# A ninth tile done by quarters in both column halves of the first feed-forward's second product, second in the order of the second half

## The chip, the cores and the metric

The kernel runs on one core of one Trainium2 chip. The metric is the device time of one execution in microseconds (us); lower is better. Times shown are the median of three runs, and a profile of one further execution.

## The reference

One decoder layer on 512 tokens of width 1024: a SwiGLU feed-forward, a token mixer (HGRN2 and mLSTM heads), a second feed-forward, each between two RMS norms and with a residual. The change lies in the first feed-forward, after `silu(gate) * up`:

```python
def swiglu_ffn(x, w_in, w_out):
    gate, up = jnp.split(x @ w_in, 2, axis=-1)
    return (jax.nn.silu(gate) * up) @ w_out
...
  x = x + 0.5 * rms_norm(swiglu_ffn(rms_norm(x, norm_pre[l, 0]), ffn1_w_in[l], ffn1_w_out[l]),
                         norm_post[l, 0])
```

`ffn1_w_out` is 2816 x 1024. The second product is therefore (512 x 2816) by (2816 x 1024).

## The kernel before

**Numbers.** All products are of float32 data, split into two float32r parts: a high part, made by a cast on ScalarE (ACT), and a low part, what is left of the value, made by a subtraction on VectorE (DVE). A product of two such operands is three matmuls: high by high, high by low, low by high. Weights are split by `split` (line 294 the cast, line 296 the subtraction) into one of four buffers, `w`; activations by `two_parts` (lines 884 and 885).

**The second product** (`ffn_out`) takes the 2816 rows of the weights in eleven tiles of 256 rows, numbered 0 to 10, and the 1024 output columns in two halves of 512. `OUT` gives the order of the tiles in each half. A tile is done in one of two ways.

- Plainly (`plain`, line 1004): 48 matmuls of 128 x 256, one weight item. The activations are split by `h_tile` into a buffer of the ring `s`, which has three.
- By quarters (`quartered`, line 1012): the tile's 2 x 2 blocks are multiplied with seven block products in place of eight (Winograd's form of Strassen's algorithm), 42 matmuls. It takes two weight items: three of the four weight quarters (a split of 768 columns), and four sums of weight quarters. The activations need three quarters, split on their own (`h_quarters`), and four sums (`h_sums`, line 919, three DVE operations), split by `s_tile` into a buffer of the ring `s`. `QUARTERED` names the tiles done so in each half.

In a half, the seven products of all quartered tiles go to four accumulators common to them (`M`) and four of the output (`C`), eight PSUM banks in all. After the half's last quartered tile, `common` combines the four `M` banks with one ACT copy and four DVE operations (lines 1039 and 969), and `add` adds the results to `C`. After the first half, eight post steps on DVE (line 491) read `C` for the norm. In the second half the last four tiles of the order (`LAST`: 0, 1, 7 and 5) are done row block by row block, so that the norm of a row block can follow (`chunk`, `last`).

**The sums of weights** are made by DMA alone, in DRAM (`sums_ahead`): three copies issued by SyncE (SP; lines 938 to 940), then three accumulating DMAs issued by GpSimd (POOL; line 944), and are loaded like weights. `make_sums` begins one tile and takes each begun one a step further; it is called at every fifth product of the first feed-forward's first part from the fifteenth on, and then at every second tile of the second product's first half.

**Buffers of the activations' quarters.** Tiles 2, 4, 6 and 8 have places of their own (`PLACES`, in `xq`). Tile 3 keeps two of the three buffers of the ring `raw` from the first half until its turn in the second. Tiles 5, 7 and 9 follow each other in the third `raw` buffer and in `gpre`, high and low part. Tiles whose quarters are used in the second half too (`stay`) have their sums written in place over the activations `hf`; the others get them in `xn` (`hsum`). In the second half before, tile 9 is done plainly, seventh in the order. Tile 7's parts go over the places of 4 and 8 there (`LATER`). `more` makes the next tiles' parts ahead; at a plain tile in place seven of the second half it makes all that are left. The first weight load of the mixer uses the ring `raw`, and the next norm's gain uses `gpre`.

Each engine runs its instructions in order. The order on each engine is set by a scheduler that goes by the code's order and its own model; it is shown below where it moves.

Of the kernel before, what the change touches and what calls it, by code (L numbers as in the profile page):

```python
# [23 lines left out]
PAIRS = NF // 2  # L24
# [60 lines left out]


FIRST = (2, 3, 4, 5, 6, 7, 8, 9)
QUARTERED = {"f1": [FIRST, (2, 3, 4, 6, 8)], "f2": [FIRST, (2, 3, 4, 6, 8, 9, 5)]}
OUT = {"f1": [list(range(PAIRS)), [10, 2, 4, 3, 6, 8, 9, 0, 1, 7, 5]]}
OUT["f2"] = [OUT["f1"][0], [10, 2, 4, 3, 6, 8, 9, 5, 7, 0, 1]]  # L90
LAST, APART, TWICE = {"f1": 4, "f2": 2}, (5, 7, 9), (5, 9)
PLACES, LATER = {2: 1, 4: 2, 6: 0, 8: 3}, {7: (2, 3)}

AGAIN, ROWS = (10,), (18, 19, 20, 21)
EVERY, EARLY, AHEAD = 5, 7, 13
# [28 lines left out]
class Layer:  # L124
# [718 lines left out]
    def ffn_in(self):  # L843

        nc = self.nc
        if not self.second:
            self.begun = ()
            self.sums_due("f1")
        for n, (p, t) in enumerate(ORDER2[len(HEADS2) :] if self.second else ORDER[len(HEADS) :]):
            if n > 14 and n % EVERY == 0 and not self.second:  # L850
                self.make_sums()
            if n == 14 and self.second:

                with self.behind(self.pooled):
                    nc.gpsimd.drain()
            with self.behind(*(self.c22 if p in ("p3", "p5") and self.second else ())):
                self.feed()
            self.c22 = []
            self.lag()
            self.prod(p, t)  # L860
            self.after(p, t)
            if t == PAIRS - 1 and p in ("p3", "p7"):
                self.hs.append(self.h_tile(len(self.hs)))
            if n == 1 and not self.second:
                self.lower_bound()
        self.feed()
        self.lag()
# [96 lines left out]
    def ffn_out(self, gpost_row, scale, after, trans, head):  # L964
# [3 lines left out]
        nc, mm = self.nc, self.nc.tensor.matmul  # L968
        tt = lambda out, a, b, op: nc.vector.tensor_tensor(out, a, b, op=op)
        f = "f2" if self.second else "f1"  # L970
        OF, QF, LF = OUT[f], QUARTERED[f], LAST[f]
        low = self.low
        seq = [(half, k2) for half in range(2) for k2 in OF[half]]
        made = deque((h, None) for h in self.hs)
# [1 line left out]
        kept, again = {}, deque()  # L976

        def more(n):
            while count[0] < min(n, len(seq)):
                half, k2 = seq[count[0]]  # L980
                count[0] += 1
                if k2 in QF[half]:
                    if k2 not in kept or half and k2 in TWICE:
                        stay = k2 in QF[1] and k2 not in TWICE
                        a = self.h_quarters(k2, PLACES.get(k2))
                        with self.behind(*([] if stay else [low])):
                            kept[k2] = a, self.h_sums(k2, stay)
                    a, f = kept[k2]
                    made.append((a, self.s_tile(f)))
                elif half and k2 in AGAIN:  # L990
                    made.append(again.popleft())
                else:
                    made.append((self.h_tile(k2, self.x_place(*LATER[k2]) if half and k2 in LATER else None), None))
                    if not half and k2 in AGAIN:
                        again.append(made[-1])
# [63 lines left out]
        n = 0  # L1059
        for half in range(2):  # L1060
            C = [[self.ps() for _ in range(2)] for _ in range(2)]
            M, T, left = None, None, len(QF[half])
            for m, k2 in enumerate(OF[half][: PAIRS - LF * half]):
                more(n + 2)
                h, sums = made.popleft()
                if sums:
                    begin = M is None
                    if begin:
                        M = {p: self.ps() for p in ("p1", "p5", "p7", "p6")}

                    quartered(C, M, h, sums, begin, half and OF[1][m : m + 2] == list(TWICE)[::-1])
                    left -= 1
                    if left == 0:
                        T = common(M, [self.hf[:, j, :] for j in ROWS] if half else [self.st("c") for _ in range(4)])
                else:
                    w = self.pull()
                    more(len(seq) if half and m == PAIRS - LF - 1 else n + 3)
                    for i in (0, 2, 1, 3):
                        for v in range(2):
                            plain(C, w, h, i, v, m == 0)  # L1080
                        if i > 1 and T and m == PAIRS - 1:
                            add(C, T, i % 2)
                    self.drop(w)
                n += 1
                if half == 0 and n % 2:
                    self.make_sums()
                if n == 1:
                    self.prod("p4", PAIRS - 1)
                    self.after("p4", PAIRS - 1)
                self.lag()  # L1090
            if half == 0:
                ys = [self.post0(pieces(C, i), g, scale) for i in range(NT)]
                self.holes()
# [884 lines left out]
```

## Time and profile before

| | us |
|---|---|
| median of three runs | 914.87 (914.43 to 915.07) |
| the profiled execution, its own time | 914.82 |
| its span, first to last instruction | 913.1 |
| second product, first half and second half to the end of the eighth tile | 223.16 to 309.5 |
| tiles 7, 8, 9, 10 of the first half begin at | 260.56, 265.32, 270.08, 274.85 |
| tiles 2, 4, 3, 6, 8, 9 of the second half begin at | 285.73, 290.5, 295.25, 300.0, 304.8, 309.52 |
| first row block of tiles 0, 1, 7, 5 begins at | 314.96 |
| head of the mixer's products (L560) begins at | 338.85 |

Times inside are microseconds from the start of the span. TensorE is PE, its weight loads PEld. A row of the timeline gives the start, the length, the engine, the line, the operation, output and input by the program's names, and how many were merged; in brackets stands the idle time before it and what ended it. A row of grouped instructions gives the busy time, the mean length of one in ns, and the idle time before them. A row of stretches gives PE, PEld, DVE, ACT and POOL busy, the granted PE clock, the DMA engines' share and GB/s.

### The profile page before, as it was taken

Reading aid. Unit: us, or ns where it says so; the run is one execution under the profiler, and the core shown is the slowest. Engines: PE = TensorE matmul, PEld = TensorE weight load, DVE = VectorE, ACT = ScalarE, POOL = GpSimd, SP = SyncE. Lnnn points to the kernel's source line nnn. Section 1 sums busy time; section 2 is a strip of 40 time slices with the busy share of each in tenths; the row PEclk is TensorE's granted clock in tenths of the full one; section 3 lists DMA queues with packets and bytes.
Section 4 is the critical chain, followed back from the end, with each engine's and each line's share of the span. In section 5 each row is a group of like instructions: output and inputs, shape, how many; then the busy total and the mean of one; then the engine's idle time right before and its main releaser. Section 6 shows DMA issues by size and latency. Waiting matters only on the chain.

```text
span 913.1 us, 18148 instructions
## 1 busy us (share of the span) xinstructions
PE 904.7 (99%) x7330; PEld 874.7 (96%) x7330; DVE 767.1 (84%) x1005; ACT 522.3 (57%) x749; POOL 183.2 (20%) x256
## 2 busy tenths in 40 slices
PE   9999999999999999999999999999999999999997
PEld 8999999999999999998888888899999999999997
DVE  6899988889888876699986655699899889988886
ACT  7645545557566557857643345694445545757661
POOL 2541112121111047742230300313000000010002
PEclk9999999999999999999999999999999999999999
DMA  9355779775897825899953127053354445388542
GB/s 311 83 161 140 186 191 213 188 156 137 222 273 237 249 62 143 158 200 210 204 119 116 40 76 253 24 162 95 97 156 140 139 130 156 101 238 242 171 144 93
DMA packets 127921, 146.51 MB, mean 160 GB/s; under 512 B 16335, under 2 KB 100303, under 8 KB 127837
## 3 DMA queue, kind: packets, MB, share of 16 engines
q1 hardware_dynamic: 111868, 130.14, 46.8%
q0 software_dynamic: 15680, 14.69, 11.8%
q8 instruction: 57, 0.93, 0.4%
q10 hardware_dynamic: 288, 0.52, 0.2%
q14 instruction: 28, 0.22, 0.1%
HBM read 143.20 MB, written 31.48 MB: 191 GB/s over the span
## 4 chain that ended last, share of the span: by engine, by line
PE 62%; ACT 0%; DVE 0%; DVEq 0%; POOLq 0%; issue 0%; POOL 0%; ACTq 0%
PE ps L619 23%; PE ps L1012 8%; PE ps L549 6%; PE ps L198 5%; PE ps L200 5%; PE ps L199 5%; PE ps L1004 4%; PE ps L560 1%; PE ps L1441 1%; PE ps L364 1%; PE ps L1540 0%; PE ps L1742 0%; PE ps L1491 0%; PE ps L1715 0%; PE ps L1739 0%; PE ps L1505 0%
## 5 line engine op out<-in xcount | busy, mean ns | idle before, releaser
L294 ACT CAST w<-raw 128x1024 fp32r<-128x1024 f32 x246 | 250.9, 1027 | 190.6 <-PE ps L619 91.7
L296 DVE TENSOR_TENSOR w<-raw,w 128x1024 fp32r<-128x1024 f32 x246 | 299.4, 1221 | 30.7 <-ACT w L294 29.5
L619 PE MATMUL ps<-xq,w 128*128 128x256 f32 x2016 | 236.9, 277 | 0.0
L619 PEld LDWEIGHTS ps<-xq,w 128*128 128x128 f32 x2016 | 232.8, 188 | 0.0
L619 PE MATMUL ps<-sq,w 128*128 128x256 f32 x1512 | 177.6, 276 | 0.0
L619 PEld LDWEIGHTS ps<-sq,w 128*128 128x128 f32 x1512 | 174.2, 188 | 0.0
L310 DVE TENSOR_TENSOR raw<-raw,raw 128x1024 f32<-128x1024 f32 x72 | 89.8, 1252 | 7.1 <-DMA raw<-in_ffn_w_in_dram 5.6
L1012 PE MATMUL ps<-w,hs 128*128 128x256 f32 x672 | 80.9, 276 | 0.0
L1004 PE MATMUL ps<-w,hs 128*128 128x256 f32 x672 | 79.2, 276 | 0.0
L1012 PEld LDWEIGHTS ps<-w,hs 128*128 128x128 f32 x672 | 78.3, 188 | 0.0
L1004 PEld LDWEIGHTS ps<-w,hs 128*128 128x128 f32 x672 | 77.5, 188 | 0.0
L198 PE MATMUL ps<-w,xq 128*128 128x512 f32 x176 | 71.1, 404 | 0.0
L200 PE MATMUL ps<-w,xq 128*128 128x512 f32 x176 | 68.9, 392 | 0.0
L199 PE MATMUL ps<-w,xq 128*128 128x512 f32 x176 | 68.6, 390 | 0.0
L944 POOL DMA_DIRECT2D f2sums<-in_ffn_w_out_dram x15 | 20.2, 1522 | 178.6 <-DMA f2sums<-in_ffn_w_out_dram 178.1
L549 PE MATMUL ps<-xq,w 128*128 128x256 f32 x480 | 55.7, 278 | 0.0
L549 PEld LDWEIGHTS ps<-xq,w 128*128 128x128 f32 x480 | 54.9, 188 | 0.5 <-issue 0.5
L884 ACT CAST hs<-hf 128x1024 fp32r<-128x1024 f32 x32 | 33.7, 1053 | 27.4 <-PE ps L1012 19.7
L885 DVE TENSOR_TENSOR hs<-hf,hs 128x1024 fp32r<-128x1024 f32 x32 | 39.1, 1223 | 9.0 <-ACT hs L884 8.4
L944 POOL DMA_DIRECT2D f1sums<-f1sums x26 | 22.0, 847 | 108.6 <-DMA f1sums<-in_ffn_w_out_dram 57.4
L944 POOL DMA_DIRECT2D f2sums<-f2sums x30 | 26.3, 911 | 85.7 <-DMA f2sums<-in_ffn_w_out_dram 44.6
L310 POOL TENSOR_TENSOR raw<-raw,raw 128x1024 f32<-128x1024 f32 x12 | 32.6, 2722 | 40.9 <-DVE w L296 40.7
(263 smaller groups left out, 1234.2 us busy)
## 6 DMA issues: line engine op xcount, KB each, us to landing
raw<-in_ffn_w_in_dram SPq DMA_DIRECT2D x98, 512.0 KB, 4.7
raw<-in_ffn_w_out_dram SPq DMA_DIRECT2D x44, 512.0 KB, 5.5
raw<-in_w_mix_in_dram SPq DMA_DIRECT2D x28, 512.0 KB, 4.7
raw<-f2sums SPq DMA_DIRECT2D x15, 512.0 KB, 5.1
raw<-f1sums SPq DMA_DIRECT2D x13, 512.0 KB, 6.4
raw<-in_w_mix_out_dram SPq DMA_DIRECT2D x8, 512.0 KB, 4.3
f2sums<-in_ffn_w_out_dram SPq DMA_DIRECT2D x30, 128.0 KB, 4.9
f2sums<-in_ffn_w_out_dram SPq DMA_DIRECT2D x15, 256.0 KB, 6.4
```

Of the source, the lines that this page charges most:

```text
L198: mm(ps, sh, mh, start=start, stop=False, **kw)
L199: mm(ps, sh, ml, start=False, stop=False, **kw)
L200: mm(ps, sl, mh, start=False, stop=stop, **kw)
L294: nc.scalar.copy(hi, raw)
L296: self.low = nc.vector.tensor_tensor(lo, raw, hi.bitcast(F32), op=ALU.subtract)
L310: added = (nc.vector if late else nc.gpsimd).tensor_tensor(o, o, c, op=ALU.add)
L549: mm(ps[:, u0:u1], w[:, a, k, :], self.xop(k, b, u0, u1), start=k + n + m == 0, stop=k == ND - 1 and n == 2, skip_group_check=True,)
L619: self.nc.tensor.matmul(ps[:, c], wb[b][:, k, v], left[d][:, k, :], start=first and a + n + k == 0, stop=n == 2 and k == KH - 1, skip_grou ...
L885: self.nc.vector.tensor_tensor(lo, src, hi.bitcast(F32), op=ALU.subtract)
L944: nc.gpsimd.dma_start(to[:, a:b], v, accum_op=ALU.add)
L1004: mm(out, a[kk][:, i * P : (i + 1) * P], w[:, b, kk, QUARTER * v : QUARTER * (v + 1)], start=begin and c == kk == n == 0, stop=kk == 1 and ...
L1012: mm(ps[:, QUARTER * c : QUARTER * (c + 1)], A[a][:, c], B[b], start=begin and c == n == 0, stop=n == 2, skip_group_check=True,)
```

## The change

Tile 9 joins the tiles done by quarters in the second half of the first feed-forward, and stands second in its order. Its quarters and sums of the first half stay, so `TWICE`, the tiles made anew for the second half, becomes a table by feed-forward: none in the first, 5 and 9 in the second, as it was. There is one more tile of weight sums to make, and `make_sums` is called once more, at the tenth product.

```diff
-QUARTERED = {"f1": [FIRST, (2, 3, 4, 6, 8)], "f2": [FIRST, (2, 3, 4, 6, 8, 9, 5)]}
-OUT = {"f1": [list(range(PAIRS)), [10, 2, 4, 3, 6, 8, 9, 0, 1, 7, 5]]}
+QUARTERED = {"f1": [FIRST, (2, 3, 4, 6, 8, 9)], "f2": [FIRST, (2, 3, 4, 6, 8, 9, 5)]}
+OUT = {"f1": [list(range(PAIRS)), [10, 9, 2, 4, 3, 6, 8, 0, 1, 7, 5]]}
 OUT["f2"] = [OUT["f1"][0], [10, 2, 4, 3, 6, 8, 9, 5, 7, 0, 1]]
-LAST, APART, TWICE = {"f1": 4, "f2": 2}, (5, 7, 9), (5, 9)
+LAST, APART, TWICE = {"f1": 4, "f2": 2}, (5, 7, 9), {"f1": (), "f2": (5, 9)}
...
-            if n > 14 and n % EVERY == 0 and not self.second:
+            if n > 9 and n % EVERY == 0 and not self.second:
                 self.make_sums()
...
-        OF, QF, LF = OUT[f], QUARTERED[f], LAST[f]
+        OF, QF, LF, two = OUT[f], QUARTERED[f], LAST[f], TWICE[f]
...
-                    if k2 not in kept or half and k2 in TWICE:
-                        stay = k2 in QF[1] and k2 not in TWICE
+                    if k2 not in kept or half and k2 in two:
+                        stay = k2 in QF[1] and k2 not in two
...
-                    quartered(C, M, h, sums, begin, half and OF[1][m : m + 2] == list(TWICE)[::-1])
+                    quartered(C, M, h, sums, begin, half and OF[1][m : m + 2] == list(two)[::-1])
```

The order of instructions differs only between the first half's last tiles and the first row block of the last four tiles, and by the copies and accumulations of the added sums. Three places follow.

**DVE at the end of the first half, before.** `hs_3208` is the low part of tile 9's sums, `hs_3263` that of tile 10, `once_3199` the low parts of tile 9's quarters, `hs_3329` the low part of tile 2's sums for the second half; `raw_172` and `raw_173` are tile 9's two weight items, `raw_178` and `raw_179` tile 10's.

```order
L885 TENSOR_TENSOR hs_3208<-hsum_3204,hs_3208 128x1024
L296 TENSOR_TENSOR w<-raw_170_2980,w 128x1024
L296 TENSOR_TENSOR w<-raw_172_3024,w 128x768
L885 TENSOR_TENSOR hs_3263<-hf_113,hs_3263 128x1024
L885 TENSOR_TENSOR once_3199<-hf_113,once_3198 128x256
L885 TENSOR_TENSOR once_3199<-hf_113,once_3198 128x512
L296 TENSOR_TENSOR w<-raw_173_3046,w 128x1024
L296 TENSOR_TENSOR w<-raw_178_3087,w 128x1024
L885 TENSOR_TENSOR hs_3329<-hf_113,hs_3329 128x1024
L296 TENSOR_TENSOR w<-raw_179_3109,w 128x1024
```

The same place now; tile 9's sums are `hs_3214` in the first half and `hs_3335` for the second, tile 10 is `hs_3269`, tile 9's quarters are `once_3206`.

```order
L296 TENSOR_TENSOR w<-raw_170_2987,w 128x1024
L296 TENSOR_TENSOR w<-raw_172_3031,w 128x768
L885 TENSOR_TENSOR once_3206<-hf_114,once_3205 128x256
L885 TENSOR_TENSOR once_3206<-hf_114,once_3205 128x512
L919 TENSOR_TENSOR hf_114<-hf_114 128x2x128
L296 TENSOR_TENSOR w<-raw_173_3053,w 128x1024
L919 TENSOR_TENSOR hf_114<-hf_114 128x4x128
L296 TENSOR_TENSOR w<-raw_178_3094,w 128x1024
L885 TENSOR_TENSOR hs_3214<-hf_114,hs_3214 128x1024
L885 TENSOR_TENSOR hs_3269<-hf_114,hs_3269 128x1024
L296 TENSOR_TENSOR w<-raw_179_3116,w 128x1024
L885 TENSOR_TENSOR hs_3335<-hf_114,hs_3335 128x1024
```

The low part of tile 9's sums moved from ahead of its quarters to behind them, behind the second and third of the sums (L919) and behind two weight splits.

**DVE at the end of the second half, before.** L969 are the steps of `common`, then of `add`; `xq_77` is tile 7's low part, `hs_3774` that of tile 1, `hs_3779` that of tile 5, `raw_247` and `raw_249` the weights of 7 and 5.

```order
L969 TENSOR_TENSOR hf_113<-ps_3501,hf_113 128x512
L885 TENSOR_TENSOR xq_77<-hf_113,xq_76 128x1024
L969 TENSOR_TENSOR hf_113<-ps_3503,hf_113 128x512
L296 TENSOR_TENSOR w<-raw_247_3634,w 128x1024
L969 TENSOR_TENSOR hf_113<-hf_113,ps_3502 128x512
L885 TENSOR_TENSOR hs_3774<-hf_113,hs_3774 128x1024
L969 TENSOR_TENSOR hf_113<-ps_3501,hf_113 128x512
L969 TENSOR_TENSOR ps_3443<-ps_3443,hf_113 128x512
L969 TENSOR_TENSOR ps_3444<-ps_3444,hf_113 128x512
L885 TENSOR_TENSOR hs_3779<-hf_113,hs_3779 128x1024
L296 TENSOR_TENSOR w<-raw_249_3665,w 128x1024
```

Now, with `hs_3835` for tile 5, `raw_248` and `raw_249` for the weights of 7 and 5, and `ps_3449` and `ps_3450` for the accumulators of the second row block:

```order
L969 TENSOR_TENSOR ps_3450<-ps_3450,hf_114 128x512
L296 TENSOR_TENSOR w<-raw_248_3671,w 128x1024
L969 TENSOR_TENSOR hf_114<-ps_3507,hf_114 128x512
L885 TENSOR_TENSOR xq_77<-hf_114,xq_76 128x1024
L969 TENSOR_TENSOR hf_114<-ps_3509,hf_114 128x512
L296 TENSOR_TENSOR w<-raw_249_3693,w 128x1024
L969 TENSOR_TENSOR hf_114<-hf_114,ps_3508 128x512
L885 TENSOR_TENSOR hs_3835<-hf_114,hs_3835 128x1024
L969 TENSOR_TENSOR hf_114<-ps_3507,hf_114 128x512
L969 TENSOR_TENSOR ps_3449<-ps_3449,hf_114 128x512
L969 TENSOR_TENSOR ps_3447<-ps_3447,hf_114 128x512
```

The last two weight splits and tile 5's low part moved in between the steps of `common`. On PE, tile 5's four first matmuls of high parts (two for each column half) and two of tile 0 for the second row block now stand ahead of the first that reads tile 5's low part.

**SP's loads in the second half, before.** `raw_3736` is the mixer's first weight item, `gpre` the next norm's gain; `raw_190`, `raw_196` and `raw_240` are tiles 3, 6 and 8.

```order
L255 DMA raw_190_3268<-in_ffn_w_out_dram 128x2x512
L255 DMA raw_191_3290<-f1sums_3_92 128x1024
L255 DMA raw_3736<-in_w_mix_in_dram 128x8x128
L165 DMA gpre_3923<-in_norm_pre_dram 128x1024
L255 DMA raw_196_3327<-in_ffn_w_out_dram 128x2x512
L255 DMA raw_234_3447<-f1sums_6_93 128x1024
L255 DMA raw_240_3506<-in_ffn_w_out_dram 128x2x512
```

Now, with `raw_239` for tile 6 and `raw_242` for tile 8:

```order
L255 DMA raw_239_3512<-in_ffn_w_out_dram 128x2x512
L255 DMA raw_240_3534<-f1sums_6_94 128x1024
L255 DMA raw_3773<-in_w_mix_in_dram 128x8x128
L165 DMA gpre_3927<-in_norm_pre_dram 128x1024
L255 DMA raw_242_3565<-in_ffn_w_out_dram 128x2x512
L255 DMA raw_243_3587<-f1sums_8_95 128x1024
```

The mixer's first load and the gain moved from behind tile 3's loads to behind tile 6's, ahead of tile 8's.

## The prediction

> **What bounds the kernel now.** I read the page's busy line first, then TensorE's waits over the whole span, then busy time by stretches around the end of the first feed-forward.
>
> ```profile
> PE 904.7 (99%) x7330; PEld 874.7 (96%) x7330; DVE 767.1 (84%) x1005; ACT 522.3 (57%) x749; POOL 183.2 (20%) x256
> PE ps L194 <- POOL ones L172: 1.2, 1, 1.2
> PE ps L364 <- DVE xn L754: 0.5, 1, 0.5
> PE ps L619 <- ACT xq L384: 0.2, 1, 0.2
> 260.00:270.00 10.00, 10.00 (x91) 10.00 (x90) 7.97 (x9) 7.02 (x9) 2.01 (x2) 1.00 0.91 203
> 275.00:280.00 5.00, 5.00 (x47) 5.00 (x46) 4.89 (x7) 1.37 (x2) 0.42 (x1) 1.00 0.96 282
> 310.00:315.00 5.00, 5.00 (x47) 5.00 (x46) 5.00 (x6) 1.04 (x2) 0.00 (x0) 1.00 0.84 236
> ```
>
> PE is busy for 99% of the span and its longest listed wait is 1.2 us at the start. In the stretches (PE, PEld, DVE, ACT, POOL, clock, DMA share) it never rests while the second product runs, at clock 1.00. So a matmul removed there is worth its pitch, and any new PE wait costs its length; nothing else counts. DVE is nearly full at 275 to 280 and at 310 to 315: there a step that moves later on DVE can become a PE wait.
>
> **The matmuls.** The ninth tile of the second column half is done plainly now: 4 row blocks x 2 column halves x 2 contraction halves x 3 terms = 48 matmuls. By quarters it is 7 products of 6, 42.
>
> ```profile
> 274.85 11.04 PE L1004 MATMUL ps<-w,hs 128*128 128x256 f32 x96
> 285.73 1.52 PE L1012 MATMUL ps<-w,xq 128*128 128x256 f32 x12
> ```
>
> The 96 matmuls of the tenth tile (48 in each half) begin at 274.85 and the next group at 285.73: 10.88 us, 113 ns each. (The 276 ns in the groups is the length of one, not its pitch.) Six fewer save **0.68 us**. A plain tile takes 5.44 us, a quartered one 4.76.
>
> **First half: the sums of the ninth tile come later.** They are now written in place over its activations, so they must follow the casts of its quarters. These need the third `raw` buffer and `gpre`, which the seventh tile holds until its last matmul.
>
> ```profile
> 264.64 0.84 PE L1012 MATMUL ps<-w,once 128*128 128x256 f32 x6
> 270.08 1.52 PE L1012 MATMUL ps<-w,once 128*128 128x256 f32 x12
> 271.44 2.88 PE L1012 MATMUL ps<-w,hs 128*128 128x256 f32 x24
> ...
> 261.17 1.23 DVE L885 TENSOR_TENSOR hs<-hsum,hs 128x1024 fp32r<-128x1024 f32 x1 [0.59 <-ACT hs L884]
> 265.80 0.92 ACT L884 CAST once<-hf 128x256 fp32r<-128x256 f32 x2
> 267.08 1.02 DVE L885 TENSOR_TENSOR once<-hf,once 128x256 fp32r<-128x256 f32 x2
> 268.01 2.35 DVE L296 TENSOR_TENSOR w<-raw,w 128x1024 fp32r<-128x1024 f32 x2
> ...
> L919 DVE TENSOR_TENSOR hf<-hf 128x512 f32<-128x512 f32 x5 | 3.4, 693 | 0.1
> L919 DVE TENSOR_TENSOR hf<-hf 128x256 f32<-128x256 f32 x5 | 2.0, 423 | 0.1
> L884 ACT CAST hs<-hf 128x1024 fp32r<-128x1024 f32 x17 | 17.9, 1054 | 16.6 <-PE ps L1012 10.6 <-PE ps L1004 4.1 <-DVE hf L919 1.9
> L1012 PEld LDWEIGHTS ps<-w,hs 128*128 128x128 f32 x312 | 36.3, 188 | 0.0
> ```
>
> Before, their low part was done at 262.4, nine microseconds ahead of its use after 271.44. Now, in the new DVE order: the seventh tile ends at 265.48; ACT casts both pieces (0.92) to 266.4; the second low piece (about 0.69) to 267.1; the second sum (0.42, after a short handover) to 267.6; the sums' weight split (half of 2.35, so 1.17) to 268.75; the third sum (0.69) to about 269.4. Then ACT casts (1.05) to 270.4 while DVE does another split, to about 270.5; the low part (1.23) ends at 271.7. PE wants it for the third matmul after 271.44, at 271.67, and must first load it (188 ns). So the cover is gone: I take **0.2 us** of wait. It is bounded by 0 and by one further DVE operation of 1.22 in between, 1.4. PE then waits one for one, since all matmuls stand in one queue.
>
> Behind it DVE has 2.3 us of work (0.42 + 0.69 + 1.23) moved from before 263 into a full stretch. From 271.6 on come five operations of 1024 columns (1.14 each), a split of 768 (0.87) and four combination steps (0.65): the combination of the first half ends at about 280.7, and the adds to the accumulators start 1.2 us later than now, the eight post steps too.
>
> ```profile
> 279.49 2.48 DVE L969 TENSOR_TENSOR ps<-ps,c 128x512 f32<-128x512 f32 x4
> 281.87 3.65 DVE L491 TENSOR_TENSOR y<-ps,gpost 128x256 f32<-128x256 f32 x8
> ```
>
> The tenth tile's second pass asks for the first bank that the combination frees, already free when ACT has copied it, and for the last only 3.4 us (30 matmuls) after its start. At 285.7 to 285.9 the quartered part needs the first old accumulator; its last reader is the fifth of the eight post steps, ending at 281.87 + 1.2 + 5/8 of 3.65 = 285.35. I cost this at **nothing**; were the banks handed out from the other end, it would be 286.7 less 285.9, 0.8.
>
> **Second half: its end has lost the plain tile.** The combination used to run beside the plain ninth tile. Now the eighth tile takes that place in time, ends at 309.52 + 4.76 = 314.28, and the last four tiles follow at once.
>
> ```profile
> 309.52 8.32 PE L1004 MATMUL ps<-w,hs 128*128 128x256 f32 x72
> 319.04 2.88 PE L1004 MATMUL ps<-w,hs 128*128 128x256 f32 x24
> ...
> 309.83 1.22 DVE L885 TENSOR_TENSOR xq<-hf,xq 128x1024 fp32r<-128x1024 f32 x1
> 310.96 0.69 DVE L969 TENSOR_TENSOR hf<-ps,hf 128x512 f32<-128x512 f32 x1
> 316.25 1.23 DVE L885 TENSOR_TENSOR hs<-hf,hs 128x1024 fp32r<-128x1024 f32 x1
> ```
>
> The seventh tile's low part is written over the eighth's quarters, so it starts when the eighth ends: 309.83 before, 314.45 now, and all that stands behind it on DVE waits. In order: that (1.14 until the next can start) to 315.6, a combination step (2.48 / 4 = 0.62) to 316.2, the fifth tile's weight split (1.14) to 317.35, a step to 317.95, the fifth tile's low part (1.23) to 319.2. Before, that was ready at 317.5 and wanted at 319.04. Now PE has done tiles 0, 1 and 7 of the first row block (36 x 113 ns) at 318.36, four high-part matmuls and two of the next block by 319.04, and then needs it, loaded, at 319.4: **0.25 us** after a rounding down, since the first wait shifts both sides alike. The add that the next block needs comes after two more steps, at 320.5, when the 11 matmuls in between have just passed. Bounds: 0, and one more DVE operation late, 1.5.
>
> **Costed at nothing.** The extra weight item makes one more 768-wide split.
>
> ```profile
> L296 DVE TENSOR_TENSOR w<-raw,w 128x768 fp32r<-128x768 f32 x13 | 12.4, 955 | 1.4 <-ACT w L294 1.1
> L294 ACT CAST w<-raw 128x768 fp32r<-128x768 f32 x13 | 10.8, 834 | 4.5 <-PE ps L1012 2.1 <-ACT w L294 1.5 <-DMA raw<-in_ffn_w_out_dram 0.8
> 295.85 1.23 DVE L885 TENSOR_TENSOR hs<-hf,hs 128x1024 fp32r<-128x1024 f32 x1 [1.30 <-ACT hs L884]
> 64.78 0.60 SPq L940 DMA_DIRECT2D f1sums<-in_ffn_w_out_dram  x1
> 65.48 0.53 SPq L255 DMA_DIRECT2D raw<-in_ffn_w_in_dram  x1
> 74.73 0.37 SPq L255 DMA_DIRECT2D raw<-in_ffn_w_in_dram  x1
> 75.55 0.84 POOL L944 DMA_DIRECT2D f1sums<-f1sums  x1 [3.82 <-DMA f1sums<-in_ffn_w_out_dram]
> 85.61 2.48 DVE L310 TENSOR_TENSOR raw<-raw,raw 128x1024 f32<-128x1024 f32 x2
> raw<-in_ffn_w_out_dram SPq DMA_DIRECT2D x44, 512.0 KB, 5.5
> ```
>
> The split's 0.96 us on DVE and 0.83 on ACT fit the 1.30 that DVE idles within a quartered tile; without it, at most 0.96. The three more copies on SP stand between the loads at 65.48 and 74.73, a gap of 9 us for about 1.8 of issuing (0.60 each); the load ahead of them is first read at 85.6, 20 us after its issue, so sharing the DMA engines with them is harmless. POOL's three more accumulations (0.84 each) fall between waits of 3 us and more on DMAs; the other tiles' keep their places because the making of sums begins one call earlier. If this cover failed, a DVE wait of a few microseconds near 70 would meet a full DVE.
>
> **Sum.** 914.82 for the profiled execution (span 913.1 and 1.7 around it; the median shown is 914.87) - 0.68 + 0.2 + 0.25 = 914.6, a gain of 0.2 us.
>
> **Rivals.** A measurement of this kernel tells about 0.2% from no change, 1.83 us.
>
> A: both low parts come in time, because handovers are shorter than I took them: 914.82 - 0.68 = 914.1, and the same verdict. For it: each lateness is some 0.2 us on a chain of five to seven operations. Against: both chains run through a full DVE.
>
> B: DVE slips by one operation at both places, or the accumulators come late too: -0.68 + 1.4 + 1.5 = +2.2 at the worst, about +1.2 in the middle, 916.0.
>
> C, slower: SP's queue blocks. The first mixer weight load now stands ahead of the eighth tile's weights in SP's order and waits for a `raw` buffer.
>
> ```profile
> 275.12 0.42 SPq L255 DMA_DIRECT2D raw<-in_w_mix_in_dram  x1
> 275.59 2.67 SPq L165 DMA_DIRECT2D gpre<-in_norm_pre_dram  x1
> 293.48 6.35 SPq L255 DMA_DIRECT2D raw<-in_ffn_w_out_dram  x4
> 905.00:913.10 8.10, 1.85 (x17) 1.66 (x15) 3.95 (x8) 0.95 (x4) 2.19 (x5) 0.83 0.52 192
> ```
>
> Now that load goes at 275.12, right after the ninth tile's buffer came free at 274.85. If it gets the ninth's buffer again, free at 290.5, the loads behind it go near 293.5 as now. If it gets one of the third tile's two, free only at 304.8, the eighth tile's weights go at 305 or later, land 5.5 later, need about 2 of splitting, and are due at 309.5: a PE wait of 3 or more, about 4 with `gpre` (2.67) ahead: 914.1 + 4 = 918. It decides where the buffer is free later than about 302. Against it: `gpre`, held by the ninth tile alone, stands right behind in the order, as it did at 275.59.
>
> The last stretch shows the granted clock at 0.83 where PE runs only 1.85 of 8.1 us. The Trainium skill, "TensorE: Matmul & The Clock Gate" (Part 1: The HAM clock gate), says the clock halves after an idle window of about 3.4 us and needs about as long to recover. By that page C would cost a further 1.7 us as an estimate, some 920, and the 0.2 us waits of my sum nothing further; the trace agrees that idleness lowers the clock, but shows no such gap in mid-kernel.
>
> D: the change doesn't do what it says: the tile stays plain. The instruction order excludes it.
>
> **Chances.** Forecast 0.50 (914.6), A 0.29 (914.1), B 0.12 (916.0, a quarter of it above 916.7), C 0.06; something not seen that gains over 1.83 us, 0.03. The range reaches from A with the spread of the runs to B: 913.8 to 916.3. Faster 0.03; slower C and a quarter of B, 0.09; same 0.88.
>
> **What would show it.** PE L1012 has 42 more and L1004 48 fewer matmuls. In the timeline PE shows a gap near 271.6, released by DVE hs L885, of 0 to 0.5, and one near 319, from the same line; the SP load of the mixer weights falls near 290.6 and not 304.8; the `f1sums` loads are 14. The forecast fails if the gaps pass 1 us, if PE waits near 286 on L491, or if later stages, whose order is untouched, change length.

## The result, and the profile after

| | before | after |
|---|---|---|
| median, us | 915.08 (914.43 to 915.49, 8 runs) | 923.23 (917.55 to 924.2, 8 runs) |
| the profiled execution, us | 914.82 | 923.19 |
| its span, us | 913.1 | 921.5 |
| matmuls | 7330 | 7324 |

The ratio is 1.0077, with a 95% interval of 1.0063 to 1.0091: the change makes the kernel 8 us slower. Six runs lie between 922.9 and 924.2, two at 917.55 and 917.74; all are above every run of before.

First the busy line and two of TensorE's waits after the change.

```profile
PE 908.7 (99%) x7324; PEld 877.8 (95%) x7324; DVE 766.5 (83%) x1006; ACT 523.8 (57%) x750; POOL 189.0 (21%) x259
PE ps L1672 <- DVE pT L1634: 3.9, 1, 3.9
PE ps L560 <- ACT w L294: 0.3, 1, 0.3
```

The six matmuls are gone, and one wait of 3.9 us is new. It explains less than half of the loss, so the rest must stand where the profile calls TensorE busy. The timeline of TensorE from tile 9's first product with a sum on shows it:

```profile
271.65 3.08 PE L1012 MATMUL ps<-w,hs 128*128 128x256 f32 x24
274.57 0.87 PE L1012 MATMUL ps<-w,once 128*128 128x256 f32 x6
275.28 11.47 PE L1004 MATMUL ps<-w,hs 128*128 128x256 f32 x96
286.58 1.58 PE L1012 MATMUL ps<-w,once 128*128 128x256 f32 x12
```

The same rows took 2.88, 0.84, 11.04 and 1.52 before. The 96 matmuls of tile 10 last from 275.28 to 286.58, 11.30 us or 117.7 ns each, where it was 113.3. No row has a wait in brackets. The stretches say the same: busy time full, clock 1.00, but fewer matmuls in five microseconds (45 where 47 stood). The last two rows belong to the mixer.

```profile
275.00:280.00 5.00, 5.00 (x45) 5.00 (x44) 5.00 (x7) 1.77 (x2) 0.69 (x1) 1.00 0.87 240
310.00:315.00 5.00, 5.00 (x45) 5.00 (x44) 4.10 (x5) 3.54 (x4) 0.00 (x0) 1.00 0.87 247
487.00:491.00 4.00, 0.44 (x8) 0.25 (x6) 0.41 (x1) 0.00 (x0) 1.97 (x5) 1.00 0.31 47
491.00:495.00 4.00, 3.67 (x12) 2.90 (x13) 4.00 (x4) 0.00 (x0) 2.63 (x4) 0.58 0.15 23
```

The starts of the single matmuls show where this pace begins. In tile 9's first product with a sum one weight load waits for the low part, 0.107 us at 271.88. Up to it the matmuls start 113.3 ns apart, behind it 117.8, until the transposes near 337 (small matmuls at L364, by which TensorE turns a tile round). From 271 up to the head of the mixer, 537 matmuls go at the slower pace; before the change 23 did, nearly all after the transposes at 331. 514 more by 4.4 ns are 2.3 us.

The account up to the head of the mixer (L560, 338.85 before, 341.17 after, 2.32 later): the execution stood 0.21 later already at the start of tile 9 in the first half; six matmuls less, -0.68; the stall, +0.11; the pace, +2.3; a stall of 0.15 near 321 on tile 5's low part, +0.15; a longer wait for the mixer's first weights (0.59 in place of 0.36 from start to start), +0.23. The sum is 2.3.

In the mixer the timeline of TensorE before:

```profile
483.85 1.16 PE L1632 MATMUL ps<-qk 64*128 64x128 f32 x16
484.94 0.87 PE L1672 MATMUL ps<-ident,qk 128*128 128x128 f32 x6
489.87 1.10 PE L1693 MATMUL ps<-vm,kw 128*64 128x129 f32 x16
```

and after:

```profile
486.28 1.16 PE L1632 MATMUL ps<-qk 64*128 64x128 f32 x16
491.33 1.50 PE L1672 MATMUL ps<-ident,qk 128*128 128x128 f32 x6 [3.89 <-DVE pT L1634]
...
493.06 0.63 PE L199 MATMUL ps<-w,xq 128*128 128x512 f32 x1
...
497.21 0.39 PE L198 MATMUL ps<-w,xq 128*128 128x512 f32 x1
497.98 1.10 PE L1693 MATMUL ps<-vm,kw 128*64 128x129 f32 x16
```

From L1632 to L1672 it was 1.09 and is 5.05, 3.96 more; from L1672 to L1693 it was 4.93 and is 6.65, 1.72 more. The second loss is the clock: 0.58 in the stretch behind the wait, with matmuls of 0.63 us that take 0.39 later. The trace's record of the clock has it at one half for 3.4 us from 491.7 on, and half of that is 1.7. The Trainium skill, "TensorE: Matmul & The Clock Gate" (Part 1: The HAM clock gate), says that the clock halves after an idle window of about 3.4 us and is full again after a busy one of about that length; the trace agrees, with a wait of 3.89 and 3.4 at one half. With 2.43 from earlier, 2.43 + 3.96 + 1.72 = 8.11 of the 8.37 us are found at L1693.

DVE's step waited for GpSimd. GpSimd (POOL) and the DVE step before:

```profile
472.56 0.81 POOL L944 DMA_DIRECT2D f2sums<-f2sums  x1 [2.82 <-DMA f2sums<-f2sums]
473.16 1.51 POOL L1624 TENSOR_SCALAR_AFFINE_SELECT e<-e 128x512 f32<-128x512 f32 x2
...
481.89 1.28 DVE L1634 SCALAR_TENSOR_TENSOR pT<-ps,e 128x512 f32<-128x512 f32 x2
```

and after:

```profile
489.03 0.81 POOL L944 DMA_DIRECT2D f2sums<-f2sums  x1 [2.77 <-DMA f2sums<-f2sums]
489.63 1.51 POOL L1624 TENSOR_SCALAR_AFFINE_SELECT e<-e 128x512 f32<-128x512 f32 x2
...
490.59 1.29 DVE L1634 SCALAR_TENSOR_TENSOR pT<-ps,e 128x512 f32<-128x512 f32 x2 [9.55 <-POOL e L1624]
```

The selects stand in GpSimd's queue behind 39 accumulating DMAs for the second feed-forward's weight sums, each of which waits for an earlier DMA. In both kernels it is 39; the last is issued 16.5 us later than before.

### The profile page after: what moved, and what is told of

It is laid out like the page before. It is cut to its first block, busy times and chain, and to the rows that moved or that the text cites. A ratio compares the mean times of both kernels' runs of the same rounds, so it can differ in the third digit from the quotient of the medians.

```text
span 921.5 us, 18154 instructions
## 1 busy us (share of the span) xinstructions
PE 908.7 (99%) x7324; PEld 877.8 (95%) x7324; DVE 766.5 (83%) x1006; ACT 523.8 (57%) x750; POOL 189.0 (21%) x259
## 4 chain that ended last, share of the span: by engine, by line
PE 53%; DMA 3%; DVE 2%; issue 2%; ACT 1%; POOL 0%; POOLq 0%; DVEq 0%; ACTq 0%
PE ps L619 23%; PE ps L1012 8%; PE ps L549 5%; PE ps L1004 4%; PE ps L198 3%; PE ps L200 3%; PE ps L199 3%; DMA f2sums<-in_ffn_w_out_dram 2%; PE ps L560 1%; PE ps L364 1%; DMA raw<-in_w_mix_in_dram 1%; DVE qk L1608 0%; PE ps L1742 0%; PE ps L1715 0%; DVE w L296 0%
## 5 line engine op out<-in xcount | busy, mean ns | idle before, releaser
L294 ACT CAST w<-raw 128x1024 fp32r<-128x1024 f32 (+1 forms) x247 | 252.2, 1029 | 206.8 <-PE ps L619 90.2
L296 DVE TENSOR_TENSOR w<-raw,w 128x1024 fp32r<-128x1024 f32 (+1 forms) x247 | 302.2, 1227 | 29.7 <-ACT w L294 28.6
L619 PE MATMUL ps<-xq,w 128*128 128x256 f32 x2016 | 236.9, 277 | 0.0
L619 PEld LDWEIGHTS ps<-xq,w 128*128 128x128 f32 x2016 | 232.8, 188 | 0.0
L619 PE MATMUL ps<-sq,w 128*128 128x256 f32 x1512 | 177.5, 276 | 0.0
L619 PEld LDWEIGHTS ps<-sq,w 128*128 128x128 f32 x1512 | 174.2, 188 | 0.0
L944 POOL DMA_DIRECT2D f1sums<-f1sums x28 | 24.8, 887 | 112.5 <-DMA f1sums<-in_ffn_w_out_dram 53.2
```

Of the source, the lines that this page charges most:

```text
L294: nc.scalar.copy(hi, raw)
L296: self.low = nc.vector.tensor_tensor(lo, raw, hi.bitcast(F32), op=ALU.subtract)
L619: self.nc.tensor.matmul(ps[:, c], wb[b][:, k, v], left[d][:, k, :], start=first and a + n + k == 0, stop=n == 2 and k == KH - 1, skip_grou ...
L944: nc.gpsimd.dma_start(to[:, a:b], v, accum_op=ALU.add)
```

## The experiments

Three questions: what sets the slower pace, what makes the mixer wait, and what else the change costs. All times are medians with the lowest and highest run; the kernel before, run beside them, had medians of 914.61 to 915.09. The diffs give the lines that matter; a condition that picks out one tile stands in the caption or the text.

**The stall taken away.** e1 takes the changed kernel and moves two matmuls; e2 gives tile 9's sums a buffer of their own again.

```diff
 e1, in product, for tile 9's S(3) of the first half alone:
+cn.sort(key=lambda f: f[1] == 2)        # low part's matmuls last
 e2, in more:
-kept[k2] = a, self.h_sums(k2, stay)
+kept[k2] = a, self.h_sums(k2, stay and k2 != 9)
```

> The changed kernel, but in tile 9's first product with a sum (first column half) the two matmuls that read the low part come fifth and sixth, not third and sixth. Nothing else moves, on any engine. The late low part was 104 ns late for the third; it is 120 ns early for the fifth. Theory 1 (the short stall of one weight load puts TensorE into a slower pace of 117.8 ns a matmul, in place of 113.3, which lasts until the transposes near 337): no stall, pace 113.3 ns throughout, the head of the mixer (L560) starts at 338.4 to 338.8 in place of 341.17, total 914.0 to 914.8. Theory 2 (the slower pace comes from where the new order puts weights and activations in SBUF): pace stays 117.8 from 272 on, L560 near 341, total about 923.

> The changed kernel, but tile 9's sums are written to the buffer that the others use (xn), so they need not follow the casts of its quarters, and their low part is ready some 9 us early as before the change. Theory 1 (stall sets the pace): pace 113.3, L560 at 338.4 to 338.8, total 914.0 to 914.8. Theory 2 (placement): pace 117.8 from 272 on, total about 923.

TensorE in e1, the same groups as above:

```profile
271.87 2.88 PE L1015 MATMUL ps<-w,hs 128*128 128x256 f32 x24
274.59 0.84 PE L1015 MATMUL ps<-w,once 128*128 128x256 f32 x6
275.27 11.04 PE L1004 MATMUL ps<-w,hs 128*128 128x256 f32 x96
286.15 1.52 PE L1015 MATMUL ps<-w,once 128*128 128x256 f32 x12
```

The pace is 113.3 again, up to the transposes. Weights, activations and every other instruction stand as in the changed kernel, so placement in SBUF is not the cause; one late weight load is. The totals were missed: e1 918.93 (six runs from 915.83 to 917.07, six from 920.79 to 923.46), e2 916.99 (eight from 916.2 to 917.92, two at 922), and L560 started at 339.80, not 338.8. Of that 0.43 stood already at tile 9 of the first half, as profiled executions differ by some tenths in when they get there (they do so at 50 us already). From there to L560 e1 takes 0.52 longer than the kernel before, though six matmuls (0.68) are gone. So the mixer's loss is there without the slow pace, in some runs, and 1.2 us of new waits has a third cause.

**A stall put into the kernel before.** e3 made one matmul wait for a DVE step.

```diff
+if self.nth == 12:                       # twelfth matmul of tile 10, first half
+    self.tc.add_manual_dep(ins, step2, Sync)
```

> The kernel before, with one wait added and no instruction moved: the twelfth matmul of tile 10 in the first half also waits for the second step of the combination on DVE (its end is near 276.10, the weight load is due at 275.98), a stall of 0.1 to 0.25 us. Theory 1: from 276 to the transposes near 331 the pace is 117.8 ns, 485 matmuls by 4.5 ns = 2.2 us more; L560 at 341.2 in place of 338.85; total 917.3 or more, and near 923 if a later arrival alone makes the mixer wait. Theory 2: pace unchanged, total 915.0 to 915.4, the stall alone.

915.28 (914.23 to 916.75), pace unchanged. This tells nothing: in that execution the DVE step had ended 0.4 us before it was asked for, and no gap stands there. The next four make the stall by a round trip: matmul n releases a one-element memset on GpSimd, and matmul n + k waits for it, at six places in the second half.

```diff
+if self.nth in TRIPS:
+    m = nc.gpsimd.memset(self.nhalf[:, 7:8], -0.5)   # waits for this matmul
+    self.tick[self.nth + TRIPS[self.nth]] = m        # that matmul waits for m
```

> The kernel before, with six short stalls put into TensorE's stream in the second half and no instruction moved: at six places, 42 matmuls apart from 286 on, one matmul releases a one-element memset on GpSimd (idle there), and a matmul 10, 9, 8, 7, 6 and 5 further on waits for it. The round trip is not known; each matmul less makes the stall 113 ns longer, so that the first may be none and the last some hundred ns. Theory 1 (a short stall sets the slower pace): 113.3 ns up to the first stall, 117.8 from there to the transposes near 331, 0.19 us more for every 42 matmuls; if it is set at the third place (294), 1.5 us and the stalls more. Rival 1b (only some stalls do, by their length): the pace changes, also back, at some places and not at others. Theory 2 (placement): 113.3 throughout, and only the stalls are added.

> The same with the longest stall first (5, 6, 7, 8, 9 and 10 matmuls). Theory 1: 117.8 from the first place (286) to the transposes near 331, 400 matmuls by 4.5 ns = 1.8 us and the stalls, 917 or more. Rival 1b: the pace is set by the length of the last stall before it, and differs from the other run's at the same place. Theory 2: 113.3 throughout.

Only k = 5 gave a stall: 0.093 us at 310.50 in s_up, 0.032 at 286.62 in s_down. The next 72 matmuls, in s_up and then in s_down:

```profile
309.60 8.70 PE L1022 MATMUL ps<-w,hs 128*128 128x256 f32 x72
```

```profile
309.55 8.32 PE L1022 MATMUL ps<-w,hs 128*128 128x256 f32 x72
```

The stall of 0.093 left 117.8 ns (8.70 holds it and 63 slower matmuls), the one of 0.032 left 113.3. s_up took 916.2, in two groups of five: 915.1 to 915.9 and 916.5 to 917.5; s_down 915.38 (914.32 to 915.66). In the profiled execution of s_up (917.4) the slow pace also outlived the transposes: it held to about 404, where TensorE stood 2.5 us later than in the kernel before. A stall alone makes the pace, in the kernel before too.

> The kernel before with six round trips of 4, 3, 2, 1, 4 and 3 matmuls to GpSimd, 42 matmuls apart from 286 on; by the earlier two (5 matmuls: 32 and 93 ns) the stalls are about 0.15 to 0.2, 0.27, 0.38, 0.5, and shorter by 4.5 ns a matmul where the pace is slow. Theory 1: slow pace (117.8) from the first stall on to the transposes near 331, whatever follows. Rival 1b (the pace after a stall goes by its length): 0.1 to 0.3 us leaves the slow pace, 0.4 to 0.5 the fast one (stalls of 0.09 to 0.25 left the slow one so far, 0.44 the fast one), so slow, slow, fast or slow, fast, slow, slow.

> The same with 1, 2, 3, 4, 5 and 5 matmuls. Theory 1: slow from the first stall on. Rival 1b: fast after the first (0.5), fast or slow after the second (0.4), slow from the third on, in the same way as the same lengths in the other run.

Here I was wrong about the lengths. In s_long all six stalls left the fast pace; two rows of it, the first with a stall of 0.32 in it:

```profile
290.06 2.54 PE L1031 MATMUL ps<-w,xq 128*128 128x256 f32 x18
292.43 2.88 PE L1031 MATMUL ps<-w,hs 128*128 128x256 f32 x24
```

In s_long2 the first four did so too, the fifth (0.093) left the slow pace, and the sixth (0.07, met at the slow pace) the fast one again:

```profile
305.60 2.31 PE L1031 MATMUL ps<-w,xq 128*128 128x256 f32 x18
307.74 2.99 PE L1031 MATMUL ps<-w,hs 128*128 128x256 f32 x24
...
319.56 1.52 PE L1022 MATMUL ps<-w,xq 128*128 128x256 f32 x12
```

The gaps between the starts of single matmuls sort them. A stall that shows as one gap of 0.09 to 0.11 us left the slow pace each time (four: the changed kernel, e4, s_up, s_long2). A longer lateness shows as two gaps, the second of 0.107 to 0.110, and left the fast pace 17 times of 18 (all such stalls within the second product that met the fast pace, here and in the runs below). Outside the second product this sorting fails. At the head of the mixer, where TensorE waits for new weights, two gaps led to either pace; near 662, in the second feed-forward (L619), where TensorE waits for an accumulator (DVE's L638, in the traces that name it), two gaps left the slow pace in e2, e5 and e8 and the fast one in e4 and e7, and single gaps of 0.05 (s_down) and 0.09 (e6) left the slow one. So the length of a stall isn't shown to decide in general. s_long's twelve gaps add up to 2.0 us, and its median is 916.78, 1.9 above the kernel before: these stalls cost their length and no more.

If that is so within the second product, a longer wait at the place of the change must be cheaper. e8 is e5 (below) with the low part's matmuls first, so that TensorE asks for it 0.226 us earlier:

```diff
-cn.sort(key=lambda f: f[1] == 2)
+cn.sort(key=lambda f: f[1] != 2)
```

> e4 (one tile of sums fewer in the mixer) with the stall made longer in place of shorter: in tile 9's first product with a sum the two matmuls that read the late low part come first, not third and sixth. TensorE asks for it 226 ns earlier, so it waits some 0.33 us in place of 0.10. Theory 1c (what the round trips showed: a lateness of about 0.1 us in one gap leaves the slow pace, a longer one, which shows as two gaps of which the second is 0.108, the fast pace): gaps of 0.2 and 0.108 near 271.4, pace 113.3 afterwards, L560 at 339.6 to 340.1, total 915.8 to 916.5, a gain of some 1.5 us on e4 by a longer wait. Rival (every stall leaves the slow pace, or the pace belongs to the placement): 117.8 as in e4, total 917.6 to 918.0.

```profile
270.23 1.52 PE L1015 MATMUL ps<-w,once 128*128 128x256 f32 x12
271.81 3.00 PE L1015 MATMUL ps<-w,hs 128*128 128x256 f32 x24
275.33 11.04 PE L1004 MATMUL ps<-w,hs 128*128 128x256 f32 x96
```

Gaps of 0.222 and 0.110, then 113.3, and L560 at 339.88, as expected; in e4, with the short stall, it was at 340.87. The total, 917.55 (916.64 to 918.79), misses the 915.8 to 916.5 that I expected, and its median is no better than e4's. The profiled run (917.05) lies 0.4 below e4's: of the 1.0 gained up to L560, 0.45 is lost again from 642 to 699, where e8 runs at the slower pace and e4 doesn't. Four of nine runs lie at 918.2 to 918.8. Whether the stall fell shorter in those is not known, for they have no trace.

**The mixer.** e4 makes one tile of the second feed-forward's sums fewer there; e5 is e1 and e4 together.

```diff
-EVERY, EARLY, AHEAD = 5, 7, 13
+EVERY, EARLY, AHEAD = 5, 7, 12
```

> The changed kernel, but one tile of the second feed-forward's weight sums fewer is made during the mixer (12 in place of 13; it is made in that feed-forward's own second product). Tests the second loss alone: theory M (POOL's queue holds the mixer's memset and selects behind the accumulating DMAs, so that TensorE waits 3.9 us at L1672 and then runs 3.4 us at half clock, 1.7 us more): with three accumulations fewer ahead, the wait falls below 1 us, the half clock at 492 is gone, total 917.4 to 917.9; the pace of 117.8 at 272 to 337 stays. Rival (the wait comes from the data of the mixer, not from POOL's queue): wait 3 to 4 us, half clock, total about 923.

> The changed kernel with both losses mended: the low part's two matmuls last (as e1) and one tile of sums fewer in the mixer (as e4). If these are the two losses and they add, all runs lie where e1's faster runs did, 915.8 to 916.3, with no wait at L1672 and pace 113.3; it stays 0.8 to 1.0 above the kernel before by the stall near 319 (0.55) and the longer wait at the head of the mixer (0.64) less the six matmuls (0.68). If e1's slower runs had another cause than the queue on GpSimd, some runs stay near 922.

TensorE in e4, then GpSimd's first selects, then the stretch that was at clock 0.58:

```profile
275.00 11.47 PE L1004 MATMUL ps<-w,hs 128*128 128x256 f32 x96
```

```profile
469.71 1.51 POOL L1624 TENSOR_SCALAR_AFFINE_SELECT e<-e 128x512 f32<-128x512 f32 x2
```

```profile
491.00:495.00 4.00, 4.00 (x34) 2.70 (x32) 3.18 (x8) 0.60 (x1) 0.00 (x0) 1.00 0.26 54
```

The slow pace is untouched, the selects come at 469.7, the wait and the half clock are gone: 917.61 (917.26 to 917.93), 5.6 us less. The two low runs of the changed kernel, 917.55 and 917.74, lie there. e5 gave 916.25 (915.64 to 917.97), no run near 922, though five of eleven lie above the 916.3 that I expected at most: the two losses are separate and both mended.

Why does the queue end so late? Not by a later start of everything: in s_long the queue started 2.0 us later than before and the memset of `vm` behind it came 2.5 later. Three runs tell the addresses in DRAM from the queue's phase: g1 is the kernel before with one unused tile more among the sums in DRAM, between those of the two feed-forwards; g2 is the kernel before with the queue started later, g3 is e1 with the queue started earlier.

```diff
 g2, behind the mask selects:
+    self.selected = nc.gpsimd.memset(self.sT, 0.0)
 g3:
-    nc.gpsimd.memset(self.sT, 0.0)
     self.masks(ma, mb)
+nc.vector.memset(self.sT, 0.0)
```

> The kernel before, with one unused tile of sums more in DRAM between those of the first and of the second feed-forward, as the change has it; no instruction differs. Theory A (addresses): the memset of vm on GpSimd at 483 to 490 in place of 473, with 26 to 28 accumulations done by 440 in place of 31; some or all runs near 920.6. Rival P (the queue's start against the other DMAs): vm at 472 to 475, 31 by 440, total 914.3 to 915.5.

> The kernel before, with a second memset of sT (1.8 us) on GpSimd between the last mask select and the first accumulation, so that the queue alone starts 1.8 us later, at 372.7. Theory P: the queue falls out of step with the other DMAs, 26 to 28 accumulations done by 440, the memset of vm at 480 to 488, TensorE waits in some runs (then 918 to 921). Theory A, or no theory: vm 2 us later, at 475, 31 by 440, total 914.3 to 915.5.

> e1 with the memset of sT on DVE in place of GpSimd, which lets the mask selects start while GpSimd waits for a DMA, so that the queue starts some 3 to 4 us earlier (about 369). Theory P: 31 accumulations by 440 or more, vm at 470 to 474, no wait at L1672, all runs 915.6 to 917 as e5. Theory A: the queue is as slow, vm at 480 to 485 (its start is earlier, its pace the same); a wait in fewer runs than e1's 6 of 12, if any.

g1: 914.62 (914.18 to 915.49, and one run at 917.55 that has no trace), `vm` at 472.9, 31 accumulations by 440. The addresses are not it. GpSimd in g2:

```profile
371.69 1.81 POOL L1812 MEMSET sT<- 128x2048 f32 x1
373.45 4.72 POOL L944 DMA_DIRECT2D f2sums<-in_ffn_w_out_dram  x4
```

The queue starts 2.6 us later than in the profile before (1.8 of it the memset), and `vm` comes at 479.7, 6.6 later, with 28 accumulations by 440: late as expected, though TensorE did not yet wait (915.26, 914.49 to 916.09). g3's queue starts at 365.2, has done 31 by 440, and `vm` comes at 477.9, where e1 had 487.6 (I expected 470 to 474); no wait at L1672. Its total, 918.07 (916.32 to 919.01), is spoiled by a new wait of 0.8 us near 352 that the memset on DVE brings. So a queue that falls back against the other DMAs loses more than its delay. Each of the three is one traced execution, and e1's runs in two groups suggest that the queue can end early or late in one kernel, so this is supported and not shown. In the changed kernel the queue starts 5.0 us later, 375.8: TensorE is 2.3 late at L560, GpSimd's first mask select is 3.9 late, and the mask selects take 14.0 us in place of 12.6. That this is what delays its queue is read from the trace alone, and why they take longer is open.

**The third part.** In e5 the pace up to the mixer and the mixer itself are as before the change, and it is still 1.2 us slower. Of the 2.0 by which its profiled execution is slower, 0.45 stood already at tile 9, the stretch from there to L560 adds 0.54, and the stretch from 642 to 699 another 0.9, where 150 matmuls go at the slower pace (last section). The 0.54 belongs to the change's place: two waits there, less the six matmuls. These waits are shown first, then for the same place a DVE row of the kernel before and three of e1:

```profile
319.93 2.90 PE L1004 MATMUL ps<-w,hs 128*128 128x256 f32 x23 [0.27 <-DVE hs L885]
...
339.83 2.42 PE L560 MATMUL ps<-xq,w 128*128 128x256 f32 x19 [0.73 <-ACT w L294]
```

```profile
319.93 1.38 DVE L969 TENSOR_TENSOR ps<-ps,hf 128x512 f32<-128x512 f32 x2 [1.31 <-PE ps L1004]
```

```profile
318.63 1.22 DVE L885 TENSOR_TENSOR hs<-hf,hs 128x1024 fp32r<-128x1024 f32 x1
319.76 0.69 DVE L969 TENSOR_TENSOR hf<-ps,hf 128x512 f32<-128x512 f32 x1
320.37 1.89 DVE L969 TENSOR_TENSOR ps<-ps,hf 128x512 f32<-128x512 f32 x3
```

Between starts the stall is 0.55 (the bracket shows 0.27 of it), and L560 waits 1.0 in place of 0.36. In e1 DVE is busy without a gap from 310.6 to 322.3; before the change it rested 1.31 us ahead of 319.93. The adds for the first row block end late, its norm follows late, and ACT splits the mixer's first weights behind that norm. Two experiments take DVE work away:

```diff
 e6 (e5), tile 7's weights of the second half:
-    self.low = nc.vector.tensor_tensor(lo, raw, hi, op=ALU.subtract)
+    nc.gpsimd.tensor_tensor(lo, raw, hi, op=ALU.subtract)
 e7 (e5), tile 7's activations of the second half:
-    self.nc.vector.tensor_tensor(lo, src, hi, op=ALU.subtract)
-    return hi, lo
+    return hi, hi
```

> e5, with the low part of tile 7's weights made on GpSimd (idle there, some 2.7 us) in place of DVE. Tests what is left: theory D (DVE is full from 306 to 322 because the combination has lost the plain tile beside it, so the adds and the norm's chain of the first row block come 0.65 us late): DVE has 1.14 us less, the stall near 319 falls from 0.55 to below 0.1, the wait at L560 from 0.9 to about 0.3, total 914.7 to 915.2. Rival (the chain waits for TensorE or ACT): stall and wait stay, total as e5, about 916.

> e5, but tile 7's low part in the second half isn't made (its high part is read twice in its place): one DVE operation of 1.14 us less between 315 and 316.3, nothing moved to another engine. Theory D (DVE is full there): the stall near 319 goes from 0.55 to below 0.2, the wait at L560 from 0.9 to 0.2 to 0.4, total about 1.1 below e5: 914.9 to 915.3. Rival (the adds and the norm's chain wait for something else): total as e5, 916.

e6: 916.58 (915.56 to 917.5), no gain. GpSimd's operation in e6, and the DVE operation that began beside it:

```profile
313.12 2.43 POOL L297 TENSOR_TENSOR w<-raw,w 128x1024 fp32r<-128x1024 f32 x1 [26.68 <-ACT w L294]
```

```profile
314.76 1.88 DVE L888 TENSOR_TENSOR xq<-hf,xq 128x1024 fp32r<-128x1024 f32 x1
```

DVE's subtraction took 1.88 us in place of 1.22 beside it, tile 5's low part came no earlier, and the stall grew to 1.0 us and here left the slow pace (the one exception of 18). The wait at L560 did fall to 0.30. e7, where the work is gone and not moved: 915.12 (914.5 to 916.74), 1.1 below e5 as expected (0.9 when each is set against the kernel before run beside it, and 0.95 by the traces from tile 9 to L560); the stall is 0.17, L560 waits 0.44. Two DVE rows of e7:

```profile
315.60 1.22 DVE L886 TENSOR_TENSOR hs<-hf,hs 128x1024 fp32r<-128x1024 f32 x1
...
320.95 0.43 DVE L501 TENSOR_TENSOR hf<-ps,gpost 128x256 f32<-128x256 f32 x1
```

Tile 5's low part is made at 315.60 where e1 had 318.63, and the norm's first step begins at 320.95 in place of 322.26; 0.37 of each is e1's later arrival at tile 9. In e7 a weight split (1.1) stands behind the low part in place of ahead, so the shorter stall is due to this order too. DVE's work is the third cause. Even so e7, which leaves out a part that the kernel needs, only draws level with the kernel before; no version with this change that was run beats it.

By medians, then: 923.23 to 917.61 is the mixer (5.6), 917.61 to 916.25 the pace (1.4, and 1.5 by the traces of e4 and e5 from tile 9 to L560; less than 2.3, since a TensorE that comes later waits less at 319 and at L560), 916.25 to 915.1 DVE.

## Why the prediction was wrong, step by step

**The matmuls.** Right in number (7330 to 7324), and 0.68 us was saved at the pace of before.

**The wait in the first half.** Forecast 0.2, measured 0.11: mechanism, place and size were right. What failed is the sentence that priced it, "any new PE wait costs its length; nothing else counts", and with it the 113 ns taken for every later matmul. The wait of 0.11 cost 2.3 us more by the pace behind it. The trace of before held the hint: after the transposes at 331.29 its rows are 0.87 for six matmuls in place of 0.84, again with no wait:

```profile
333.57 0.87 PE L1004 MATMUL ps<-w,xq 128*128 128x256 f32 x6
```

The prediction quoted no timeline row of TensorE behind 322.

**Behind it on DVE.** Right: no wait stands near 286.

**The end of the second half.** The place was right, the size not: 0.25 forecast, 0.15 in the changed kernel, where TensorE comes late itself, and 0.55 in e1 and e5. In e1 DVE reached tile 7's low part at 315.17, not at 314.45 (0.43 of that is the later arrival at tile 9), because a weight split and a step of the combination stood before it. The step that was left out is the first row block: I followed the adds only to the next block's matmuls (320.5), not to the first block's norm and on to ACT and L560. That was rival B's "accumulators come late", at another reader.

**The queue of SP.** Right: the mixer's first load went at 291.61, and no weights came late. Rival C did not occur.

**Costed at nothing.** The copies and accumulations of the added sums brought no wait of TensorE near 70; tile 9 of the first half starts within 0.21 us of before.

**Later stages.** This is the larger failure: "later stages, whose order is untouched" were taken to keep their length, and 5.7 us arose in one. The order was the same; the time at which GpSimd's queue starts against the DMAs was not, and nothing in the prediction asked how much room the mixer's waits had: before, GpSimd's first selects started at 473.16 and DVE's step that reads them at 481.89; with the selects at 489.63 that room was gone. No rival covered it. The price of a long gap, 1.7 us of half clock, was given for rival C, and it is what the mixer paid.

## What to carry to other kernels

A full TensorE is no proof that it runs at its pace: count matmuls per microsecond in the stretches, before and after, and look at the first row that is longer than its twin. A dependency that arrives 0.1 us late in a long gapless stream can cost twenty times that, so give it room or move the matmuls that need it by two places. And where an engine's queue mixes waits on DMAs with work that the bound engine reads, ask how late that work may be before a change upstream is called free.

## What the runs showed of the hardware

- TensorE had two stable paces for the same 128 x 256 matmuls at full clock: 113.3 and 117.8 ns. In the first feed-forward's second product, one weight load late by 0.09 to 0.11 us led from the first to the second, in four of four cases; lateness of 0.15 us or more, seen as two gaps, kept the first in 17 of 18. The eight transposes at L364 led to either. What inside the engine does this is not settled. The Trainium skill, "TensorE: Matmul & The Clock Gate" (Back-to-back issue gap), says that the spacing of such pairs is set by the weight load and the matmul together; no run here takes the two apart. The runs show two spacings for one shape, and that a late weight load alone leads from one to the other (e1, s_up).
- The same happened elsewhere: 150 matmuls from 662 on ran at the slower pace in the profiled executions of e2, e5, e6, e8 and s_down, and not in those of the kernel before, e1 and g3, 0.67 us. Stalls of 0.05 to 0.36 us led to it, three of them with two gaps. The runs of the kernel before that stand in the first table spread over 1.06; whether this pace is why is not shown.
- A wait of 3.44 us in e1 was followed by a half clock too:

```profile
489.32 1.54 PE L1675 MATMUL ps<-ident,qk 128*128 128x128 f32 x6 [3.44 <-DVE pT L1637]
```

- Beside a GpSimd subtraction of 128 x 1024, a DVE subtraction of the same size took 1.88 us in place of 1.22 (e6, one case).
